# Softmax maxima of a hybrid attention layer: split into two float16 parts before the turn, and turned by a float16 product

## The chip, the cores and the metric

The kernel runs on one core of a Trainium2 chip. The metric is the device time of one execution in microseconds (us), as the median over runs. Before the change it is 2776.42 us, the median of three runs between 2773.62 and 2778.46.

The engines are named as in the profile: PE is TensorE (matrix products; PEld are its weight loads), DVE is VectorE, ACT is ScalarE, POOL is GpSimd, SP is SyncE, which issues most of the transfers. PSUM is the memory that TensorE writes to, in banks of 128 partitions by 512 float32 numbers; SBUF is the main on-chip memory.

## What is computed

The reference is one transformer layer over 2048 tokens of width 1024: a modulated RMS norm, a projection, bidirectional retention beside an attention with 8 query heads and 2 key heads, an output projection, and a feed-forward block. The change lies in the attention alone:

```python
def _dense_attention(q, k, v):
    s = jnp.einsum('bqkgd,bskd->bkgqs', q, k).astype(jnp.float32) * ATT_SCALE
    p = jax.nn.softmax(s, axis=-1).astype(v.dtype)
    return jnp.einsum('bkgqs,bskd->bqkgd', p, v)
```

There are 2304 keys (256 of the context, 2048 of the sequence), head size 64. The softmax subtracts the maximum of each query's scores. The queries and keys are multiplied as split float16 numbers (a high part and the remainder, the low part).

## The kernel before

**Stages.** A first stage (to about 636 us) normalizes and projects the tokens and writes queries, keys and values to memory. The second stage (636 to about 1560 us) is the attention, with the retention, the output projection and the first steps of the feed-forward block between its steps. The third stage (to the end) is the feed-forward block.

**Attention groups.** The attention runs over 32 groups: 16 tiles of 128 queries by 2 key heads, each group with 4 query heads. A group has two passes over the keys.

- *Maxima.* `piece` multiplies queries (as weights, queries on the output's partitions) with 512 keys at a time into a PSUM bank named "mp" (L172, and L176 for the last 256 keys). There are 18 pieces in a group. `maximum` (L185, DVE) reduces each piece to the negated maximum of each query and puts it into the tile "nm". `least` (L191, DVE, twice) takes the minimum of the five parts for each head; it writes the same numbers to columns 64 and 96 of a tile "mt" (queries on partitions, four heads).
- *Turn.* `turn` (L196, PE) transposes "mt" for each of the four heads into an "mp" bank, so that the minima lie along one partition. `rows` (L199, ACT) copies partitions 64 to 127 of that bank as float16, scaled, into the second half of the query tile "qr". `rows2` (L203, DVE) then replaces partitions 96 to 127 by the remainder that float16 had cut off. With them the scores' product subtracts the maximum by itself.
- *Scores and values.* `scores` multiplies 128 keys (as weights) with the 512 queries into a bank "st" (L209 and L210; L210 uses the rows above). `exp` (L215, ACT), `cast` (L219, ACT) and `low` (L226 on POOL or L228 on DVE) make the high and low float16 parts of the probabilities, and `values` (L242, L243) multiplies them with the values.

**Order.** A table of events sets the order. Group n begins its pieces at step k = 18n, one piece a step, and its scores at step k + 22. In each step the phases run in the order scores, piece, maximum, early, exp, cast, low, chain, values and some others for the work between. `least` stands in the chain phase of step k + 18, `turn` in the piece phase of step k + 19 (ahead of the next group's second piece), `rows` in the cast phase of step k + 20 and `rows2` in the early phase of step k + 21. The passes of two groups overlap: while group n turns its minima, group n + 1 makes its first pieces and group n - 1 its last scores.

**Banks.** There are two "mp" banks. Pieces of all groups and the turns share them. A bank is given again when all that reads it is done; which of the two a tile gets is decided when the program is built, by a model of the time. The program's wait for a bank is a semaphore of the engine that read it last.

## Time and profile before

| | |
|---|---|
| median of three runs | 2776.42 us (2773.62 to 2778.46) |
| the profiled execution, first to last instruction (its span, and the only time that the page gives of it) | 2774.9 us |
| TensorE busy | 2657.9 us, 96% |
| VectorE busy | 2103.3 us, 76% |
| ScalarE busy | 1600.3 us, 58% |
| GpSimd busy | 1423.2 us, 51% |
| granted TensorE clock, mean | 0.989 of full speed |

A row of a time line gives the start in us, the duration in us, the engine, the line of the kernel, the operation, the tiles written and read, the sizes, and in brackets how long the engine was idle before and what released it. A row of stretches gives a stretch's bounds and length, then busy time and instructions of PE, PEld, DVE, ACT and POOL, the granted clock, the share of the transfer engines and GB/s. A row of waits gives who waited for what: us in total, times, the longest. Matmuls are pipelined and their ends are modelled, so how long one holds TensorE is read from the start of the next.

### The profile page before, as it was taken

The numbers are of one execution on the slowest core, as the hardware profiler recorded it, in microseconds if no ns is written. First come the engines' busy times: TensorE is split into PE (matmuls) and PEld (weight loads), VectorE is DVE, ScalarE is ACT, GpSimd is POOL, SyncE is SP. The second block draws the span as 40 slices with busy tenths as digits, with TensorE's granted clock in tenths as the row PEclk, the third lists the DMA queues.
The fourth block names the chain that finished last, engine by engine and source line by source line (L and its number), as shares of the span: only waits on it lengthen the run. The fifth ranks groups of instructions, "written<-read, shape, count | busy, mean of one in ns | idle before, by whom it ended". The sixth has DMA issues, their size and how long they took to land.

```text
span 2774.9 us, 45229 instructions
## 1 busy us (share of the span) xinstructions
PE 2657.9 (96%) x16896; PEld 1432.6 (52%) x16896; DVE 2103.3 (76%) x3306; ACT 1600.3 (58%) x2736; POOL 1423.2 (51%) x1182
## 2 busy tenths in 40 slices
PE   7999999888999999999999889999999999999998
PEld 2545654445666666666666544444444444444443
DVE  5857677668877777777777577989999956666676
ACT  3633762227877777787778576555554564434442
POOL 2623772365755657676667644454556721111155
PEclk9999999999999999999999999999999999999999
DMA  7478758584111231322222665665657332222223
GB/s 265 132 251 294 225 167 271 150 265 169 48 60 53 67 96 57 98 79 86 86 76 83 239 209 175 204 190 179 200 187 273 129 108 83 84 89 79 84 76 137
DMA packets 275045, 402.51 MB, mean 145 GB/s; under 512 B 107717, under 2 KB 163141, under 8 KB 272522
## 3 DMA queue, kind: packets, MB, share of 16 engines
q1 hardware_dynamic: 271802, 394.90, 43.9%
q10 hardware_dynamic: 3024, 4.72, 0.5%
q8 instruction: 133, 2.18, 0.3%
q14 instruction: 86, 0.70, 0.1%
HBM read 294.54 MB, written 105.00 MB: 144 GB/s over the span
## 4 chain that ended last, share of the span: by engine, by line
PE 76%; DVE 11%; DMA 4%; issue 3%; ACT 3%; POOL 2%; SPq 0%; POOLq 0%; ACTq 0%; DVEq 0%
PE pd L1894 6%; PE pd L1892 6%; PE pd L1893 6%; PE pu L1715 6%; PE pu L1717 6%; PE pu L1716 6%; PE pso L650 5%; PE pso L651 5%; PE pso L652 5%; PE o L243 3%; PE st L209 3%; PE st L210 3%; PE mp L172 3%; DVE plo L228 2%; DVE nm L185 2%
## 5 line engine op out<-in xcount | busy, mean ns | idle before, releaser
L185 DVE TENSOR_REDUCE nm<-mp 128x1 f32<-128x512 f32 (+1 forms) x576 | 390.3, 685 | 158.6 <-PE mp L172 131.4
L215 ACT ACTIVATE p<-st 128x512 f32<-128x512 f32 x576 | 339.1, 599 | 178.1 <-PE st L210 122.5
L226 POOL TENSOR_TENSOR plo<-p,phi 128x1024 f16<-128x1024 f32 x160 | 351.4, 2197 | 173.2 <-ACT phi L219 141.7
L1715 PE MATMUL pu<-hf,w1f 128*128 128x512 f16 x896 | 341.0, 381 | 7.2 <-ACT w L1732 3.8
L1717 PE MATMUL pu<-hf,w1f 128*128 128x512 f16 x896 | 341.0, 381 | 0.0
L1716 PE MATMUL pu<-hf,w1f 128*128 128x512 f16 x896 | 340.7, 380 | 0.0
L219 ACT ACTIVATE phi<-p 128x1024 f16<-128x1024 f32 x288 | 304.1, 1056 | 0.0
L651 PE MATMUL pso<-wlo,h 128*128 128x512 f16 (+1 forms) x816 | 296.2, 363 | 2.0 <-DVE wlo L548 2.0
L650 PE MATMUL pso<-whi,h 128*128 128x512 f16 (+1 forms) x816 | 296.5, 363 | 1.3 <-ACT whi L547 1.3
L652 PE MATMUL pso<-whi,h 128*128 128x512 f16 (+1 forms) x816 | 296.0, 363 | 0.0
L228 DVE TENSOR_TENSOR plo<-p,phi 128x512 f16<-128x512 f32 x256 | 235.1, 919 | 16.1 <-ACT phi L219 14.9
L242 PE MATMUL o<-wv,plo 128*128 128x65 f16 x2304 | 234.9, 193 | 13.0 <-POOL plo L226 6.6
L243 PE MATMUL o<-wv,phi 128*128 128x129 f16 x2304 | 242.7, 220 | 0.0
L242 PEld LDWEIGHTS <-plo 128*128 128x128 f16 x2304 | 206.1, 98 | 55.6 <-POOL plo L226 15.9
L1918 DVE SCALAR_TENSOR_TENSOR acc<-pd,scv,acc 128x512 f32<-128x512 f32 x248 | 183.1, 743 | 54.0 <-PE pd L1894 51.4
L209 PE MATMUL st<-qr,ks 128*128 128x512 f16 x576 | 219.6, 381 | 4.4 <-ACT p L215 3.8
L210 PE MATMUL st<-qr,ks 128*128 128x512 f16 x576 | 219.7, 381 | 0.1
L243 PEld LDWEIGHTS <-phi 128*128 128x128 f16 x2304 | 205.2, 97 | 21.3 <-issue 0.5
L172 PE MATMUL mp<-ks,qr 128*128 128x512 f16 x512 | 196.1, 383 | 17.2 <-DVE nm L185 17.0
L1680 POOL TENSOR_TENSOR w1s<-w1r 128x512 f32<-128x512 f32 x64 | 92.4, 1444 | 233.4 <-ACT w L1754 159.9
L1892 PE MATMUL pd<-w2t,us 128*128 128x512 f16 x496 | 188.0, 379 | 1.7 <-DVE acc L1918 1.7
L1893 PE MATMUL pd<-w2t,us 128*128 128x512 f16 x496 | 188.0, 379 | 0.0
(377 smaller groups left out, 6109.2 us busy)
## 6 DMA issues: line engine op xcount, KB each, us to landing
w2t<-w2f SPq DMA_DIRECT2D x98, 512.0 KB, 4.2
wm<-in_w_ff SPq DMA_DIRECT2D x64, 512.0 KB, 5.0
w1r<-in_w_ff SPq DMA_DIRECT2D x64, 512.0 KB, 4.7
w2f<-w2f SPq DMA_DIRECT2D x98, 256.0 KB, 2.4
wmr<-in_w_mod SPq DMA_DIRECT2D x32, 512.0 KB, 5.3
w2r<-in_w_ff SPq DMA_DIRECT2D x32, 512.0 KB, 4.2
hf<-hp SPq DMA_DIRECT2D x56, 256.0 KB, 3.5
hf<-hf SPq DMA_DIRECT2D x14, 1024.0 KB, 7.2
```

Source lines behind the costliest of these rows:

```text
L185: nc.vector.tensor_reduce(dst, src, axis=AX.X, op=ALU.max, negate=True)
L226: nc.gpsimd.tensor_tensor(lo, p, hi, op=ALU.subtract)
L242: mm(o[:, : HD + 1], lo[:, i, c], v[:, : HD + 1], start=False, stop=False)
L243: mm(o, hi[:, i, c], v[:, :VW], start=False, stop=last)
L650: mm(self.ps[:, c], hi[:, k], wh, start=k == 0, stop=False)
L651: mm(self.ps[:, c], hi[:, k], wl, start=False, stop=False)
L652: mm(self.ps[:, c], lo[:, k], wh, start=False, stop=k == KT - 1)
L1715: mm(pu[c], whi, hi, start=first and k == 0, stop=False, **more)
L1716: mm(pu[c], whi, lo, start=False, stop=False, **more)
L1717: mm(pu[c], wlo, hi, start=False, stop=k == 3, **more)
L1892: mm(ps, uh, wh, start=first and j == 0, stop=False, **more)
L1893: mm(ps, uh, wl, start=False, stop=False, **more)
```

## The change

The minima are split into a float16 high part and a low part while the queries still lie on partitions, 4 numbers to each partition. `least` now makes three steps on VectorE: one reduction into a small tile "ml", the high part (L192, scaled, rounded to float16 in "mt", column 64), and the low part (L193, the scaled minimum less the high part, column 96). "mt" is a float16 tile, the turn is an ordinary product with a float16 identity, and ScalarE's copy takes both parts at once. `rows2` is gone.

```diff
         def least(self, mt):
             self.mt = mt
             nm = self.nm.rearrange("p a b c -> p (a b) c")
-            for c in (64, 96):
-                nc.vector.tensor_reduce(mt[:, :, c], nm, axis=AX.X, op=ALU.min)
+            m = sm.tile([P, 4], F32, name="ml", tag="ml")
+            nc.vector.tensor_reduce(m, nm, axis=AX.X, op=ALU.min)
+            nc.vector.tensor_scalar_mul(mt[:, :, 64], m, 1 / ROW)
+            nc.vector.scalar_tensor_tensor(mt[:, :, 96], m, 1 / ROW, mt[:, :, 64], op0=ALU.mult, op1=ALU.subtract)
...
             for h in range(4):
-                nc.tensor.transpose(self.m[:, h], self.mt[:, h], ident)
+                mm(self.m[:, h], self.mt[:, h], ident16, start=True, stop=True)
...
-            nc.scalar.activation(self.qr[64:, 1], self.m[64:], AF.Copy, scale=1 / ROW)
-
-        def rows2(self):
-            lo = self.qr[96:, 1]
-            nc.vector.scalar_tensor_tensor(lo, self.m[96:], 1 / ROW, lo, op0=ALU.mult, op1=ALU.subtract)
+            nc.scalar.activation(self.qr[64:, 1], self.m[64:], AF.Copy)
...
+    ident16 = vp.tile([P, P], F16, name="ident16")
+    nc.vector.tensor_copy(ident16, ident)
-    mts = [vp.tile([P, 4, P], F32, name=f"mt{i}") for i in range(2)]
+    mts = [vp.tile([P, 4, P], F16, name=f"mt{i}") for i in range(2)]
...
-        nc.gpsimd.memset(mt[:, :, 80], PSHIFT * math.log(2.0) * HD**0.5)
+        nc.gpsimd.memset(mt[:, :, 80], PSHIFT * math.log(2.0) * HD**0.5 / ROW)
...
             on(k + NK + 2, "cast", g.rows)
-            on(k + NK + 3, "early", g.rows2)
```

Lines behind the diff's first part stand two lower afterwards (L228 is then L226, L226 then L224), and `rows` becomes L201; L191 is then the one reduction, L198 the turn.

The order of VectorE around the 25th turn, before. Rows are in the engine's order; "mt0" is the turned tile, "nm" the maxima, "mp" the banks, and the brackets name the engines whose semaphores a step waits for.

```order
L228 TENSOR_TENSOR plo_17049<-p32_16985,phi_17035 128x512 [waits DVE_49,Pool_49]
L191 TENSOR_REDUCE mt0_6849<-nm_16616 128x4 [waits DVE_49]
L191 TENSOR_REDUCE mt0_6849<-nm_16616 128x4
L185 TENSOR_REDUCE nm_17039<-mp_17043 128x1 [waits PE_49]
L228 TENSOR_TENSOR plo_17049<-p32_16985,phi_17035 128x512
L185 TENSOR_REDUCE nm_17039<-mp_17079 128x1 [waits PE_49]
L1543 TENSOR_TENSOR u_17103<-bank1_17092,a2_302 128x512 [waits DMAHW7_49,PE_49]
L1386 TENSOR_TENSOR oat_17130<-bank0_17087,dT_318 128x512
L185 TENSOR_REDUCE nm_17039<-mp_17100 128x1 [waits PE_49]
L203 SCALAR_TENSOR_TENSOR qr_16298<-mp_17074,qr_16298 32x512 [waits DMAHW0_49,Activation_49]
```

The same place after the change:

```order
L226 TENSOR_TENSOR plo_17075<-p32_17011,phi_17061 128x512 [waits DVE_49,Pool_49]
L191 TENSOR_REDUCE ml_17077<-nm_16641 128x4 [waits DVE_49]
L192 TENSOR_SCALAR mt0_6851<-ml_17077 128x4 [waits DVE_49]
L193 SCALAR_TENSOR_TENSOR mt0_6851<-ml_17077,mt0_6851 128x4 [waits DVE_49]
L185 TENSOR_REDUCE nm_17065<-mp_17069 128x1 [waits PE_49]
L226 TENSOR_TENSOR plo_17075<-p32_17011,phi_17061 128x512
L185 TENSOR_REDUCE nm_17065<-mp_17107 128x1 [waits PE_49]
L1542 TENSOR_TENSOR u_17131<-bank1_17120,a2_302 128x512 [waits DMAHW7_49,PE_49]
L1385 TENSOR_TENSOR oat_17158<-bank0_17115,dT_318 128x512
L185 TENSOR_REDUCE nm_17065<-mp_17128 128x1 [waits PE_49]
```

The two reductions, of which the second waited for nothing, became three steps that each wait for the one before (DVE's own semaphore); L203 is gone from behind the third maximum.

TensorE at the same turn, before: the turn, the first piece behind it ("mp_17079"), and the second and third ("mp_17100", "mp_17138").

```order
L196 MATMUL mp_17074<-ident_60,mt0_6849 128x128 [waits DVE_49,PE_49]
L196 MATMUL mp_17074<-ident_60,mt0_6849 128x128 x3
L172 MATMUL mp_17079<-ks_315,qr_16742 128x512 [waits DVE_49]
...
L172 MATMUL mp_17100<-ks_315,qr_16742 128x512 [waits DVE_49]
...
L172 MATMUL mp_17138<-ks_315,qr_16742 128x512 [waits DVE_49]
```

After the change:

```order
L198 MATMUL mp_17102<-ident16_6849,mt0_6851 128x128 [waits PE_49]
L198 LDWEIGHTS mt0_6851
L198 MATMUL mp_17102<-ident16_6849,mt0_6851 128x128
...
L172 MATMUL mp_17107<-ks_315,qr_16768 128x512 [waits DVE_49]
...
L172 MATMUL mp_17128<-ks_315,qr_16768 128x512 [waits Activation_49]
...
L172 MATMUL mp_17166<-ks_315,qr_16768 128x512
```

The second piece behind the turn now waits for ScalarE, the copy out of the turn's bank, and no longer for VectorE's maximum of the first piece. This is so at 25 of the 31 turns that have pieces behind them; at the other 6 the second piece still waits for VectorE and the third for ScalarE. The rest of the order of ScalarE, GpSimd and SyncE is the same.

## The prediction

> **What bounds the kernel now.** I read the page's head first, then the stretch of the attention stage, then what TensorE waits for in it, and last the time line around single turns.

> ```profile
> span 2774.9 us, 45229 instructions
> PE 2657.9 (96%) x16896; PEld 1432.6 (52%) x16896; DVE 2103.3 (76%) x3306; ACT 1600.3 (58%) x2736; POOL 1423.2 (51%) x1182
> 636.00:1520.00 884.00, 845.16 (x7913) 558.84 (x7913) 702.27 (x1233) 685.03 (x1115) 587.57 (x441) 0.99 0.25 79
> PE mp L172 <- DVE nm L185: 15.6, 23, 2.6
> PE o L242 <- DVE plo L228: 5.6, 9, 1.2
> PE o L242 <- POOL plo L226: 4.8, 7, 1.7
> PE mp L196 <- DVE mt L191: 2.6, 4, 0.7
> ```

> The third line is the stretch in which all 32 turns lie: 884.0 us, of which TensorE is busy 845.2, VectorE 702.3, ScalarE 685.0 and GpSimd 587.6. TensorE sets the pace; what the other engines save counts only where TensorE waits for them. The last four lines are those waits. The longest, L172 for L185, lies mostly right behind a turn. Here is the 14th, first TensorE, then ScalarE and VectorE:

> ```profile
> 989.38 0.60 PE L196 MATMUL mp<-ident,mt 128*128 128x128 f32 x4
> 989.82 0.38 PE L172 MATMUL mp<-ks,qr 128*128 128x512 f16 x1
> 990.25 0.38 PE L210 MATMUL st<-qr,ks 128*128 128x512 f16 x1
> 990.98 0.38 PE L172 MATMUL mp<-ks,qr 128*128 128x512 f16 x1 [0.35 <-DVE nm L185]
> 990.21 0.59 ACT L199 ACTIVATE qr<-mp 64x512 f16<-64x512 f32 x1
> 990.24 0.69 DVE L185 TENSOR_REDUCE nm<-mp 128x1 f32<-128x512 f32 x1 [0.49 <-PE mp L172]
> ```

> The four transposes hold TensorE for 989.82 - 989.38 = 0.44 us. The turn keeps one of the two "mp" banks until L203 has read it, so the second piece behind it (990.98) goes to the bank of the first piece and must wait for that piece's maximum (990.24 + 0.69 = 990.93). Going through all 32 turns in this way (from start to start on TensorE), I count about 14 us lost at the second piece.

> **The change, part by part.** *The turn on TensorE.* No row shows an fp16 product of 128 columns. The nearest is the pair of L242 (65 columns) and L243 (129):

> ```profile
> 1547.67 0.19 PE L242 MATMUL o<-wv,plo 128*128 128x65 f16 x1
> 1547.70 0.22 PE L243 MATMUL o<-wv,phi 128*128 128x129 f16 x1
> 1547.76 0.19 PE L242 MATMUL o<-wv,plo 128*128 128x65 f16 x1
> 1548.37 0.38 PE L209 MATMUL st<-qr,ks 128*128 128x512 f16 x1
> ```

> L243 holds TensorE for 1547.76 - 1547.70 = 0.06 us, its weight load beside it. So four products take about 0.23 us for 0.44, 0.21 less a turn; the other end is the fp32 rate, no gain, and nothing speaks for a loss. I take the L243 row: its type is that of the new product, its columns one more. At most 32 x 0.21 = 6.7 us, but only where nothing else holds the next piece. [...]

> *The minima on VectorE.* Before, two independent reductions; after, three steps that each wait for the one before.

> ```profile
> L191 DVE TENSOR_REDUCE mt<-nm x64: 157/166/175, 636.4 to 1518.2; 128x4 f32<-128x20 f32 x64
> L203 DVE SCALAR_TENSOR_TENSOR qr<-mp,qr x32: 696/697/698, 640.5 to 1522.3; 32x512 f16<-32x512 f32 x32
> 92.66 0.17 DVE L1034 TENSOR_SCALAR lgp<-lgp 128x8 f32<-128x8 f32 x1
> 92.86 0.17 DVE L1033 TENSOR_TENSOR lgp<-lgp,dw 128x8 f32<-128x8 f32 x1
> 93.06 0.17 DVE L1034 TENSOR_SCALAR lgp<-lgp 128x8 f32<-128x8 f32 x1
> ```

> Dependent small steps start 0.20 us apart. The pair of L191 takes 0.25 us in all (the 25th turn below shows 0.24); the new chain takes 0.20 + 0.20 + 0.17 = 0.57, so the turn's operand is ready 0.32 us later. Queued behind it on VectorE is the maximum of the first piece of the next group, for whose bank TensorE's next L172 waits. In 9 turns TensorE waits for the chain already, and the 0.32 us comes back there; in the others there are 0.3 us or more to spare.

> *A lock that the new chain meets.* Its last step reads two SBUF operands (the minimum and the high part); neither L191 nor L203 (one operand in PSUM) does. What that can cost, a tiny step of the same kind shows:

> ```profile
> L1526 DVE TENSOR_TENSOR ss<-ss x16: 130/159/2058, 792.0 to 1596.7; 128x1 f32<-128x1 f32 x16
> 1360.63 2.06 DVE L1526 TENSOR_TENSOR ss<-ss 128x1 f32<-128x1 f32 x1
> 1360.55 2.13 POOL L226 TENSOR_TENSOR plo<-p,phi 128x1024 f16<-128x1024 f32 x1
> ```

> A step of 0.16 us lasted 2.06 because GpSimd's L226 had started 0.08 us earlier; it ended with L226. L191 never left 157 to 175 ns. [...] I laid the new step (0.40 us behind the first L191) over GpSimd's rows at each turn: in 7 of 32 it falls into a running GpSimd step that lasts another 0.6 to 0.9 us. The 25th turn:

> ```profile
> 1307.76 0.24 DVE L191 TENSOR_REDUCE mt<-nm 128x4 f32<-128x20 f32 x2
> 1308.05 1.03 POOL L1356 TENSOR_TENSOR okw<-ork,kd 128x512 f32<-128x512 f32 x1
> 1308.15 0.63 PE L196 MATMUL mp<-ident,mt 128*128 128x128 f32 x4 [0.70 <-DVE mt L191]
> ```

> The new step would start at 1308.16 and wait until 1309.08, so this turn moves by 0.92 + 0.32 = 1.24 us.

> *L203 goes, the bank is free earlier.* L203 is 0.70 us of VectorE in each turn, 22.3 us in all, but VectorE is idle 884.0 - 702.3 = 181.7 us of the stretch. What counts is the bank. The order shows that in most turns the second piece now takes the turn's own bank and waits for ScalarE's copy (in the 14th: 990.21 + 0.59 = 990.80, 0.13 us ahead of the maximum; and the copy itself starts 0.21 earlier). Where the copy comes late, the scheduler left the old wait in place (6 turns). The largest loss of all, in the 26th turn, shows what is late next:

> ```profile
> 1340.18 2.46 DVE L228 TENSOR_TENSOR plo<-p,phi 128x512 f16<-128x512 f32 x1
> 1342.56 0.68 DVE L185 TENSOR_REDUCE nm<-mp 128x1 f32<-128x512 f32 x1
> 1343.29 0.59 PE L172 MATMUL mp<-ks,qr 128*128 128x512 f16 x1 [2.61 <-DVE nm L185]
> 1344.95 0.26 PE L242 MATMUL o<-wv,plo 128*128 128x65 f16 x1
> ```

> The piece no longer waits for 1343.24. The next values product, which started at 1344.95, needs the L228 that ends at 1342.64, and 0.32 us later behind the longer chain: it can start at about 1343.0, 1.9 us earlier, and no more.

> *The sum at the start of the values product behind each turn.* Fourteen turns in which the chain has room: 0.11 to 0.33 us earlier each, -3.1 us. Nine in which the chain is waited for or nearly: the eight without the 26th together +0.8, the 26th -1.9. Seven blocked by GpSimd: from -0.8 to +1.2 (the 25th), together +3.2. The last turn has no pieces behind it: 0. The first turn is covered:

> ```profile
> 640.47 0.70 DVE L203 SCALAR_TENSOR_TENSOR qr<-mp,qr 32x512 f16<-32x512 f32 x1
> 641.32 0.58 PE L209 MATMUL st<-qr,ks 128*128 128x512 f16 x1 [0.24 <-DMA qr<-aq]
> ```

> The first scores wait for the queries' transfer (641.32), not for L203 (641.17). The transfer hides both the gain there and the new identity's cast, once 0.2 us (by L1034's row); without it the first turn would be some 0.5 us later. Together -1.0 us. Other pieces that wait for L185 find VectorE 0.70 - 0.32 us less busy in each group: the total of that wait is 15.6 us, most of it at the turns, so I take -0.5 us, between 0 and -2.

> *The clock.* After two of the long waits TensorE ran at half clock:

> ```profile
> 663.66:667.07 3.41, 1.26 (x13) 0.62 (x11) 2.94 (x3) 1.70 (x3) 1.66 (x1) 1.00 0.00 0
> 667.07:670.48 3.41, 3.41 (x21) 1.76 (x19) 1.94 (x3) 1.34 (x3) 2.12 (x1) 0.50 0.02 5
> 1339.50:1342.91 3.41, 1.18 (x8) 0.65 (x7) 3.41 (x4) 3.14 (x8) 2.13 (x1) 1.00 0.63 137
> 1342.91:1346.32 3.41, 3.03 (x21) 1.93 (x21) 1.71 (x3) 1.36 (x2) 1.92 (x1) 0.50 0.91 286
> ```

> Stretches of 3.41 us in which TensorE was busy 1.26 and 1.18 us are followed by one at a granted clock of 0.50, which costs up to 1.7 us each. The waits there shrink to about 1.5 us but do not go. I count one of the two as gone, -1.7 us, with ends 0 and -3.4. Sum: -1.0 - 0.5 - 1.7 = -3.2 us. The profiled execution's span of 2774.9 us lies 1.5 below the median of 2776.42, within the three runs (2773.62 to 2778.46), so I take the sum off the median: 2773 us.

> **The rivals.** *The gain comes in full.* If GpSimd's steps shift so that the new step seldom meets one, the seven blocked turns give what the others do and the sum at the turns is -5.3; with -0.5 and one to two half-clock stretches (-1.7 to -3.4) that is about -8, 2768 us. For it: the blocked steps are 0.6 to 0.9 us from being free, and the order around them moves. Against it: GpSimd is busy 587.6 of 884.0 us. Chance 0.34.

> *Slower by the lock.* The same busy share, 0.66, would put 21 of 32 turns under a GpSimd step if the seven I count are luck. Each blocked turn costs 4.3 / 7 = 0.6 us net (the sum with it, -1.0, less the sum without, -5.3, over seven). From 19 on the loss outweighs the gains by 0.2%: 19 x 0.6 = 11.4 against 5.3 + 0.5 + 5.5. At 21, with both half-clock stretches left, it is 12.6 - 5.3 - 0.5 = +6.8 us, 2783 us. Chance 0.11.

> *The product is no faster than the transpose.* Then the fourteen free turns give nothing: -3.2 + 2.9, 2776 us. Its chance, 0.05, is in the 0.55 for no measurable change.

> **How the numbers follow.** About 0.2%, 5.5 us, is what a measurement of this kernel can tell from no change (its three runs spread over 4.8). The forecast, 2773, with the rival at 2776, has 0.55 and lies within it; the full gain, 0.34, is faster; the lock, 0.11, is slower. The range leaves out the far tenth of the one and most of the other: 2766 to 2781 us.

> **What would show it.** Right: the four L198 start 0.06 us apart and hold TensorE 0.23 us; L191 to L193 start 0.20 us apart in most turns, and in about 7 the last lasts 0.6 us or more with a GpSimd step beside it; the wait of L172 for L185 falls to some 5 us, and waits for ScalarE's copy and for the turn's operand appear, 3 to 7 us each; one half-clock stretch is left. Wrong: L193 blocked in 15 turns or more, or hardly ever; the products at 0.11 us; or the gain found outside the 884 us.

## The result: 0.36% slower

| | before | after |
|---|---|---|
| median of four runs each | 2777.06 us (2773.62 to 2778.46) | 2786.08 us (2785.47 to 2788.93) |
| ratio, with its 95% interval | | 1.0036 (1.0023 to 1.005) |
| start of the first and of the last turn | 636.80, 1519.35 | 636.53, 1527.41 |
| from the first to the last turn | 882.55 us | 890.88 us |

The forecast of 2773 us was wrong, and the time lies outside its range. Nearly the whole loss lies between the first turn and the last: 8.3 us more there, against 8.9 us more in the span (2783.8 for 2774.9). One execution among all those below (e13, 6322 us) is a slow one and enters no ratio. The page's head after the change:

```profile
span 2783.8 us, 45173 instructions
PE 2649.6 (95%) x16896; PEld 1424.7 (51%) x16896; DVE 2104.5 (76%) x3307; ACT 1598.2 (57%) x2736; POOL 1418.7 (51%) x1182
```

The stretch that holds the 32 turns:

```profile
636.00:1528.00 892.00, 839.17 (x7913) 551.51 (x7914) 708.69 (x1229) 683.66 (x1115) 584.03 (x441) 0.99 0.26 78
```

And what TensorE waits for in it (us in total, times, the longest; the prediction's rows count from 640 us, and from there on the first two totals are 12.1 and 11.0):

```profile
PE mp L198 <- DVE mt L193: 13.1, 12, 2.7
PE mp L172 <- DVE nm L185: 12.3, 26, 2.2
PE o L240 <- DVE plo L226: 9.3, 14, 1.3
PE mp L172 <- ACT qr L201: 1.1, 3, 0.4
```

TensorE works 6.0 us less in the stretch (839.2 for 845.2), as it should, and yet the stretch is 8.0 us longer. Counted from 640 us in both, the turn's wait for its operand has risen from 2.6 to 12.1 us, and the values' wait for VectorE's low part (L226, before L228) from 5.6 to 9.3. The pieces' wait for the maximum fell by only 4.6 us, from 15.6 to 11.0. VectorE lost the 22.3 us of L203, but is as busy as before (2104.5 for 2103.3): something in it takes longer. The three new steps, as minimum, median and longest in ns:

```profile
L191 DVE TENSOR_REDUCE ml<-nm x32: 156/164/170, 516.6 to 1526.2; 128x4 f32<-128x20 f32 x32
L192 DVE TENSOR_SCALAR mt<-ml x32: 175/177/1046, 636.0 to 1526.4; 128x4 f16<-128x4 f32 x32
L193 DVE SCALAR_TENSOR_TENSOR mt<-ml,mt x32: 176/177/2111, 636.2 to 1526.6; 128x4 f16<-128x4 f32 x32
```

The reduction never varies; each of the others is sometimes many times as long. The fifth turn, GpSimd and VectorE in order of time, then the turn on TensorE:

```profile
731.05 1.72 POOL L1424 TENSOR_TENSOR oo<-oo,ogate 128x512 f32<-128x512 f32 x1
731.57 0.16 DVE L191 TENSOR_REDUCE ml<-nm 128x4 f32<-128x20 f32 x1
731.76 1.05 DVE L192 TENSOR_SCALAR mt<-ml 128x4 f16<-128x4 f32 x1
732.80 2.12 POOL L224 TENSOR_TENSOR plo<-p,phi 128x1024 f16<-128x1024 f32 x1
732.84 2.11 DVE L193 SCALAR_TENSOR_TENSOR mt<-ml,mt 128x4 f16<-128x4 f32 x1
735.01 0.61 PE L198 MATMUL mp<-ident,mt 128*128 128x128 f16 x4 [2.56 <-DVE mt L193]
```

L192 has one SBUF operand, and was not on my list of steps that can be blocked. It is held until GpSimd's L1424 ends (731.05 + 1.72 = 732.77). By then GpSimd's next step is ready and starts at 732.80. L193 needs L192's result, comes at 732.84 and loses again, this time for a whole GpSimd step. A chain of 0.59 us takes 3.38 (731.57 to 734.95). No L191 lasted over 0.17 us in the 32 turns; why a step of L192's form can be held, the rows don't show.

The blocked turns and how long the two steps lasted, in us (0.18 where nothing blocks):

| turn | 5th | 19th | 23rd | 25th | 27th | 29th | 31st |
|---|---|---|---|---|---|---|---|
| L192 | 1.05 | 0.93 | 0.93 | 0.18 | 0.81 | 0.81 | 0.81 |
| L193 | 2.11 | 1.19 | 1.19 | 0.95 | 0.18 | 0.18 | 0.97 |

These are the seven turns that the prediction counted. Over 0.18 us the steps add up to 4.3 us at L192 and 5.5 at L193. In four of the six turns with a held L192, L193 is held as well. Behind two of these turns TensorE then ran at half clock:

```profile
731.54:734.95 3.41, 0.91 (x13) 0.42 (x10) 3.34 (x5) 1.67 (x3) 3.35 (x2) 1.00 0.00 0
734.95:738.36 3.41, 3.35 (x22) 2.10 (x23) 2.57 (x5) 1.89 (x3) 0.00 (x0) 0.50 0.00 0
1137.73:1141.14 3.41, 0.84 (x8) 0.65 (x9) 3.34 (x6) 1.81 (x3) 3.41 (x4) 1.00 0.38 79
1141.14:1144.55 3.41, 3.41 (x25) 2.25 (x24) 3.41 (x4) 2.04 (x3) 2.77 (x2) 0.50 0.03 7
```

Both half-clock stretches of before (667.07 and 1342.91) are gone; these two, at the 5th and the 19th turn, took their place.

A second loss has no new step in it. At the 11th turn VectorE's subtraction L228 (after: L226) is an old step with two SBUF operands, right behind the chain and the first maximum. Before, it came 0.13 us ahead of GpSimd's L226:

```profile
901.95 0.68 DVE L228 TENSOR_TENSOR plo<-p,phi 128x512 f16<-128x512 f32 x1
902.08 2.54 POOL L226 TENSOR_TENSOR plo<-p,phi 128x1024 f16<-128x1024 f32 x1 [3.59 <-DVE xr L1512]
```

After the change the longer chain makes it 0.20 us late instead, and the next maximum and the second piece wait behind it:

```profile
903.89 2.12 POOL L224 TENSOR_TENSOR plo<-p,phi 128x1024 f16<-128x1024 f32 x1 [3.59 <-ACT phi L217]
904.09 2.47 DVE L226 TENSOR_TENSOR plo<-p,phi 128x512 f16<-128x512 f32 x1
906.49 0.68 DVE L185 TENSOR_REDUCE nm<-mp 128x1 f32<-128x512 f32 x1
907.22 0.38 PE L172 MATMUL mp<-ks,qr 128*128 128x512 f16 x1 [2.18 <-DVE nm L185]
```

Whichever starts second waits: before, it was GpSimd's step, 2.54 us for 2.12; after, VectorE's, 2.47 us for 0.68. Such a VectorE step of over 2 us stands behind 2 turns before and behind 9 after, of which three (the 19th, the 25th and the 31st) are turns whose chain was itself held. So there were two theories of a lock (on the new steps, the lock theory of the expectations; on the old step that now comes late, called the race below), and as rivals the longer way to the operand by itself (the chain or operand theory), and the bank or the product (the bank theory).

### The profile page after: what moved, and what is told of

Read it like the earlier page. It is cut to its first block, busy times and chain, and to the rows that moved or that the text cites. A ratio compares the mean times of both kernels' runs of the same rounds, so it can differ in the third digit from the quotient of the medians.

```text
span 2783.8 us, 45173 instructions
## 1 busy us (share of the span) xinstructions
PE 2649.6 (95%) x16896; PEld 1424.7 (51%) x16896; DVE 2104.5 (76%) x3307; ACT 1598.2 (57%) x2736; POOL 1418.7 (51%) x1182
## 3 DMA queue, kind: packets, MB, share of 16 engines
q8 instruction: 133, 2.18, 0.3%
## 4 chain that ended last, share of the span: by engine, by line
PE 77%; DVE 11%; ACT 3%; DMA 3%; issue 3%; POOL 2%; SPq 0%; POOLq 0%; ACTq 0%; DVEq 0%
PE pu L1714 6%; PE pu L1715 6%; PE pu L1716 6%; PE pd L1893 6%; PE pd L1891 6%; PE pd L1892 6%; PE pso L648 5%; PE pso L649 5%; PE pso L650 5%; PE o L241 3%; DVE plo L226 3%; PE st L207 3%; PE st L208 3%; PE mp L172 3%; DVE nm L185 2%
## 5 line engine op out<-in xcount | busy, mean ns | idle before, releaser
L185 DVE TENSOR_REDUCE nm<-mp 128x1 f32<-128x512 f32 (+1 forms) x576 | 389.2, 684 | 159.7 <-PE mp L172 132.2
L224 POOL TENSOR_TENSOR plo<-p,phi 128x1024 f16<-128x1024 f32 x160 | 349.6, 2186 | 173.1 <-ACT phi L217 132.6
L226 DVE TENSOR_TENSOR plo<-p,phi 128x512 f16<-128x512 f32 x256 | 248.6, 972 | 19.0 <-ACT phi L217 17.8
L172 PE MATMUL mp<-ks,qr 128*128 128x512 f16 x512 | 195.1, 381 | 13.8 <-DVE nm L185 12.3
```

The costliest lines, as they stand in the source:

```text
L185: nc.vector.tensor_reduce(dst, src, axis=AX.X, op=ALU.max, negate=True)
L224: nc.gpsimd.tensor_tensor(lo, p, hi, op=ALU.subtract)
```

## Experiments

Line numbers shift by a few between the kernels. In all of them the order of ScalarE, GpSimd and SyncE is that of the kernel they are made from; TensorE's follows the banks of before where L203 stands, of after where it doesn't. Each ratio is against the kernel before on the same chip. The expectations of e1 to e4 are in us and go by the 2777 us of before in the table above; on the chip of these four, before takes 2772.7 us, so they are to be compared as ratios.

| kernel | ratio, 95% interval | first to last turn, us |
|---|---|---|
| after | 1.0036 (1.0023 to 1.005) | 890.9 |
| e1: four reductions | 0.9996 (0.9987 to 1.0004) | 878.7 |
| e2: last step alone can be blocked | 1.0010 (1.0001 to 1.0018) | 881.5 |
| e3: high part alone | 0.9983 (0.9974 to 0.9992) | 877.8 |
| e4: before, two steps that can be blocked | 1.0106 (1.0091 to 1.0122) | 908.1 |
| e5: before, two reductions instead | 1.0056 (1.0044 to 1.0069) | 899.1 |
| e6: after again | 1.0030 (1.0020 to 1.0041) | 892.1 |
| e7: e3 with float32 transposes | 0.9983 (0.9974 to 0.9992) | 876.8 |
| e8: e3 with L203 and its bank | 0.9986 (0.9977 to 0.9995) | 876.3 |
| e9: e3, two reductions behind the operand | 0.9998 (0.9989 to 1.0008) | 881.8 |
| e10: e8, two reductions behind the operand | 1.0038 (1.0025 to 1.0051) | 893.8 |
| e11: after without L193 | 1.0004 (0.9995 to 1.0013) | 881.9 |
| e12: e11 with a reduction for L192 | 0.9989 (0.9981 to 0.9998) | 878.7 |
| e13: before, one reduction for two | 0.9999 (0.9990 to 1.0008) | 882.9 |

The last column is from one profiled execution each, the start of the last turn less that of the first (before: 882.6).

**e1: the same two parts by reductions alone.**

```diff
-            m = sm.tile([P, 4], F32, name="ml", tag="ml")
-            nc.vector.tensor_reduce(m, nm, axis=AX.X, op=ALU.min)
-            nc.vector.tensor_scalar_mul(mt[:, :, 64], m, 1 / ROW)
-            nc.vector.scalar_tensor_tensor(mt[:, :, 96], m, 1 / ROW, mt[:, :, 64], op0=ALU.mult, op1=ALU.subtract)
+            m = sm.tile([P, 4, 2], F32, name="ml", tag="ml")
+            nc.vector.tensor_reduce(mt[:, :, 64], nm, axis=AX.X, op=ALU.min)
+            nc.vector.tensor_reduce(m[:, :, 0], nm, axis=AX.X, op=ALU.min)
+            nc.vector.tensor_reduce(m[:, :, 1], mt[:, :, 64:65], axis=AX.X, op=ALU.min, negate=True)
+            with nc.allow_low_precision(reason="low part"):
+                nc.vector.tensor_reduce(mt[:, :, 96], m, axis=AX.X, op=ALU.add)
...
-    nc.vector.tensor_copy(ident16, ident)
+    nc.vector.tensor_scalar_mul(ident16, ident, 1 / ROW)
...
-        nc.gpsimd.memset(mt[:, :, 80], PSHIFT * math.log(2.0) * HD**0.5 / ROW)
+        nc.gpsimd.memset(mt[:, :, 80], PSHIFT * math.log(2.0) * HD**0.5)
```

> The same two parts are formed by four reductions on VectorE and nothing else (no step with two SBUF operands, none of the form of L192); the scale 1/ROW sits in the identity. The order on TensorE, ScalarE, GpSimd and SyncE is that of the changed kernel. Lock theory (both L192 and L193 lose to GpSimd's steps, and that is the whole loss): no step of the chain lasts over 0.25 us, the turn's product waits some 4 us in all instead of 14.5, the two half-clock stretches behind the long waits are gone, 2771 to 2777 us. Chain theory (the operand is ready later because three dependent steps stand where two independent ones stood): this chain is 0.1 us longer still, so 2786 us or more. Bank theory (the second piece waits for ScalarE's copy, or the product itself costs): nothing of that changes, 2784 to 2788 us.

Measured: 0.9996. The last step:

```profile
L195 DVE TENSOR_REDUCE mt<-ml x32: 172/174/177, 632.8 to 1511.1; 128x4 f16<-128x8 f32 x32
```

And the turn's wait for it:

```profile
PE mp L200 <- DVE mt L195: 4.0, 6, 0.9
```

No step of the chain is long any more, the wait is 4.0 us, and from 641 us to the last turn there is no half-clock stretch. The loss of 0.30 to 0.36% is gone, though this chain is longer: the new steps' lock is the loss. By the chain theory or the bank theory it would have stayed. But e1 is only level with before: what the change was to gain is not there either.

**e2: only the last step can be blocked.** A second reduction of the maxima, which doesn't wait for the first, makes the high part in place of L192; the difference (`tensor_tensor`) has two SBUF operands. The scale is in the identity, as in e1.

```diff
             m = sm.tile([P, 4], F32, name="ml", tag="ml")
+            nc.vector.tensor_reduce(mt[:, :, 64], nm, axis=AX.X, op=ALU.min)
             nc.vector.tensor_reduce(m, nm, axis=AX.X, op=ALU.min)
-            nc.vector.tensor_scalar_mul(mt[:, :, 64], m, 1 / ROW)
-            nc.vector.scalar_tensor_tensor(mt[:, :, 96], m, 1 / ROW, mt[:, :, 64], op0=ALU.mult, op1=ALU.subtract)
+            nc.vector.tensor_tensor(mt[:, :, 96], m, mt[:, :, 64], op=ALU.subtract)
...
```

> L192 becomes a reduction that doesn't depend on the first; only the last step, with two SBUF operands, can be blocked. This is the case that the prediction priced: one blocked step in about 7 turns, 0.6 to 0.9 us each. Lock theory with two steps in a row (the second loses because the first was held until GpSimd started its next step): the last step is blocked for the rest of one GpSimd step only, never for two, and the time falls by more than half of the loss, 2777 to 2780 us. Lock theory with the last step alone at fault: 2785 us, as the changed kernel. Chain theory: the chain is 0.1 us shorter, 2784 us. Bank theory: 2784 to 2788 us.

Measured: 1.0010.

```profile
L193 DVE TENSOR_TENSOR mt<-ml,mt x32: 176/178/966, 633.2 to 1514.1; 128x4 f16<-128x4 f32 x32
```

Its longest is 0.97 us (six turns, 0.73 to 0.97), never a whole GpSimd step of 2.1; the two reductions ahead of it last 0.18 us at most. This is the lock that the prediction priced, at 4.3 us, and it costs 0.14% over e1, 3.9 us. The rest of the change's lock, 0.20 to 0.26%, comes with L192: its own hold, and the second collision of L193 that follows from it.

**e11 and e12: L192 alone.** In e11 only L193 and the low part are taken out; in e12 a reduction also takes L192's place.

> The changed kernel without L193: one reduction and L192, the step with one SBUF operand; the low part is left out. If a step of L192's form alone can lose to GpSimd: it lasts 0.8 to 1.05 us in 5 or 6 turns (730, 1138, 1254, 1376, 1436 and 1496 us in the changed kernel), and the time is 2 to 5 us above the same chain in reductions. If only steps with two SBUF operands are blocked and L192's delays in the changed kernel came from its neighbour: all at 0.18 us, the same time as the chain in reductions.

> Control for the last: the high part by two dependent reductions (the second in L192's place; the low part is left out), as long a chain (0.38 us) and nothing that can be blocked. Race theory: 0.13 us more of VectorE than before the change, which is about the margin by which L228 came ahead of GpSimd in the turn at 902 us, so between one and five of the lost races: 0.9983 to 0.9995. Operand theory: 0.9983 to 0.9988.

Measured: 1.0004 and 0.9989. The second fits the race's range and, by its interval, the operand's too: e12 serves as a control alone. In e11:

```profile
L192 DVE TENSOR_SCALAR mt<-ml x32: 176/177/1043, 634.8 to 1516.1; 128x4 f16<-128x4 f32 x32
```

A step with one SBUF operand on four numbers is blocked by itself, in the same six turns as in the change; 0.15% between the two, some 4 us. L192 alone and L193 alone (e2) thus cost 0.15 and 0.14%, the two in a row 0.34 to 0.40%. That this is more than their sum is what the second collision leads one to expect (behind a held L192, L193 is held for 4.7 us in all), but with intervals of some 0.1% to each side the times alone don't show the size of that share.

**e4 and e5: the same steps in the kernel before.** Two steps whose results nobody reads stand between the two reductions of L191: in e4 of the forms of L192 and L193, in e5 two reductions.

> The kernel before, with two more steps between its two reductions, of the forms of L192 and L193, whose results nobody reads; the transposes, L203 and the banks stay. Lock theory: some 5 to 9 turns have a step blocked for 0.5 to 2.1 us, 2782 to 2788 us. Chain theory (0.4 us later in the 9 turns that wait for the chain): 2780 to 2781 us. Bank theory: 2777 to 2778 us.

> Control for the kernel before with two more steps: the same two places, but both steps are reductions, which have not been blocked in any run so far. The chain is as long, nothing can lose to GpSimd. Lock theory: of the 29 us that the two steps cost there, at least 12 (the lock's cost in the first turn-to-last-turn stretch of the changed kernel) go, and no half-clock stretch follows a long wait: 1.001 to 1.006 of the kernel before. Chain theory: nothing of it goes, 1.009 to 1.011.

Measured: 1.0106 and 1.0056. The first lies far above what any of the theories gave. The difference between the two, half a per cent, is the lock:

```profile
L193 DVE SCALAR_TENSOR_TENSOR ml<-mt,ml x32: 161/164/2107, 635.0 to 1542.6; 128x4 f16<-128x4 f32 x32
```

The other half I had not foreseen when I wrote e4's ranges: two reductions of 0.16 us, of which the first never lasts over 163 ns, cost 0.56%, 15.5 us, in 32 turns. The 1.0056 lies within what e5's lock theory allowed, but its sign does not: four half-clock stretches (from 689.9, 908.3, 1085.8 and 1355.5 us) follow long waits, where none was expected. So "the lock on the new steps is all" does not hold in this kernel, and that led to the race. By itself e5 doesn't tell the race from the later operand: the turn's wait for it rises too, from 2.6 to 5.2 us.

**e6: after again.**

> The changed kernel again, beside the others on one chip: 1.0025 to 1.005 of the kernel before, the same seven turns blocked, L192 over 0.25 us in 6 and L193 in 5 of them, whatever the theory; if the blocked turns were luck of one execution, other turns or another number of them.

Measured: 1.0030, with the same longest steps (1048 and 2110 ns) in the same seven turns. The collisions are the program's, not one execution's luck. The clock is in part luck: behind the 25th turn e6 has a third half-clock stretch, after one in which TensorE was busy 1.56 of 3.41 us; in the first execution TensorE was busy 1.71 us in the stretch at that place, and no half clock followed.

**e3, e9: the operand, or what stands behind it.** e3 has one reduction into the float16 tile (scale in the identity, no low part); e9 adds two dependent reductions behind it (the edit is that from e3 to e9).

```diff
             nc.vector.tensor_reduce(mt[:, :, 64], nm, axis=AX.X, op=ALU.min)
+            d = sm.tile([P, 2, 4], F16, name="ml", tag="ml")
+            nc.vector.tensor_reduce(d[:, 0], mt[:, :, 64:65], axis=AX.X, op=ALU.min)
+            nc.vector.tensor_reduce(d[:, 1], d[:, 0].unsqueeze(2), axis=AX.X, op=ALU.min)
```

> The minimum is kept as its high part alone, by one reduction; the low part (row 96 of the rows) is left out and stays zero. Lock theory: as with four reductions, and up to 3 us less for the shorter chain, 2768 to 2775 us. Chain theory: the operand is ready 0.1 us earlier than before the change, so the whole gain of the shorter turn and of L203 shows, 2766 to 2770 us. Bank theory: 2783 to 2787 us.

> The high part alone (the low part is left out), and behind it two more dependent reductions of four values that nobody reads. TensorE's operand is ready as early as with the high part alone; what stands behind on VectorE comes 0.4 us later, as in the changed kernel where nothing is blocked. Race theory (what costs is that VectorE's subtraction L228 right behind the turn comes just after GpSimd's L226 instead of just ahead of it, and then waits for it): that step lasts over 2 us in 7 to 9 turns instead of 2, and 2 to 4 us come back: 0.9989 to 0.9998 of the kernel before. Operand theory (what costs is the later operand of the turn): no change, 0.9980 to 0.9987.

Measured: 0.9983 and 0.9998. The operand is ready as early in both (TensorE waits for it 1.9 us in all in either). The 11th turn in e3:

```profile
900.13 0.68 DVE L223 TENSOR_TENSOR plo<-p,phi 128x512 f16<-128x512 f32 x1
900.27 2.52 POOL L221 TENSOR_TENSOR plo<-p,phi 128x1024 f16<-128x1024 f32 x1 [3.60 <-DVE xr L1508]
```

And in e9:

```profile
898.20 2.13 POOL L224 TENSOR_TENSOR plo<-p,phi 128x1024 f16<-128x1024 f32 x1 [3.59 <-ACT phi L217]
898.39 2.49 DVE L226 TENSOR_TENSOR plo<-p,phi 128x512 f16<-128x512 f32 x1
901.53 0.38 PE L172 MATMUL mp<-ks,qr 128*128 128x512 f16 x1 [2.18 <-DVE nm L185]
```

VectorE comes 0.14 us first in the one and 0.19 us late in the other. The subtraction is over 2 us behind 2 turns in e3 and behind 6 in e9 (7 to 9 were expected), as in e1, which is as fast as e9. The race theory holds, the operand theory doesn't: 0.15%, 4 us, for 0.4 us of VectorE that TensorE's operand never sees. The lost races are not worth the same: in the profiled executions e9 is 4.0 us behind e3 at the last turn, and 3.9 of them arise between the 11th turn and the 12th, with the wait of 2.18 us above and a half-clock stretch behind it (from 902.2). Over the rest of the way the two are even; e3 has two half-clock stretches of its own, both before 700 us.

**e7, e8, e10: the product and the bank.** e7 is e3 with "mt" in float32 and the transposes of before. e8 is e3 with `rows2` back. e10 is e8 with e9's two reductions.

> The high part alone (the low part, row 96, is left out), but through the float32 transposes of before: the bank is free as early as with the product, only the product's gain is missing. If the shorter turn is worth what was forecast (0.21 us in some 14 to 20 turns), 3 to 4 us above the kernel with the high part alone: 0.9993 to 1.0000. If that gain is swallowed by other waits: 0.998 to 0.999, as there.

> The high part alone (the low part is left out) through the float16 product, but L203 of before stands again: it reads the turn's bank late and holds VectorE 0.70 us in each turn (it works on zeros). If the earlier bank and VectorE's time are worth something (forecast: the second piece's wait for L185 falls from 15.6 us to some 5): 3 to 8 us above the kernel with the high part alone, 0.9995 to 1.001. If other waits take that place: 0.998 to 0.999.

> The same two reductions in the kernel that keeps L203 and the late bank (high part alone, float16 product). Race theory with the bank: the second piece behind the turn then waits for a maximum that stands behind the blocked subtraction, in some six turns by 1.4 to 2.3 us, and half-clock stretches come with it: 8 to 12 us above the same kernel without the two steps, 1.0015 to 1.0035 of the kernel before. If the earlier bank is worth nothing in such turns either: 0.999 to 1.0 as with the early bank. Operand theory: 0.9983 to 0.999.

Measured: 0.9983, 0.9986 and 1.0038, the last a little above its range. With the short chain it makes no difference whether the product or the early bank is there. With the long one the bank (with L203's 0.70 us of VectorE) matters: e10 lies 0.52% above e8, e9 only 0.15% above e3. The 18th turn shows how. After the change:

```profile
1109.95 2.48 DVE L226 TENSOR_TENSOR plo<-p,phi 128x512 f16<-128x512 f32 x1
1111.39 0.38 PE L172 MATMUL mp<-ks,qr 128*128 128x512 f16 x1
```

In e10:

```profile
1109.95 2.51 DVE L230 TENSOR_TENSOR plo<-p,phi 128x512 f16<-128x512 f32 x1
1113.11 0.38 PE L172 MATMUL mp<-ks,qr 128*128 128x512 f16 x1 [1.53 <-DVE nm L185]
```

The same lost race; the second piece takes the turn's bank in the one, and in the other waits 1.7 us longer for a maximum behind the blocked subtraction. So the change's early bank did work: it hid most of the races that the change's own chain lost. It is also the likely reason for e5's loss, as e5 has the late bank.

**e13: the kernel before with one reduction for two.**

```diff
-            for c in (64, 96):
-                nc.vector.tensor_reduce(mt[:, :, c], nm, axis=AX.X, op=ALU.min)
+            nm = bc(nm.unsqueeze(2), [P, 4, 2, 5])
+            nc.vector.tensor_reduce(mt[:, :, 64:128:32], nm, axis=AX.X, op=ALU.min)
```

> The kernel before, whole, with one reduction in place of the two of L191: it reads the maxima twice (a repeated dimension) and writes both columns of the turned tile. Transposes, L203, banks and the order of every engine stay. If what the three kernels with the high part alone gain (0.9983 to 0.9986) comes from what they have in common with this one, the VectorE steps ahead of the turn taking 0.17 instead of 0.25 us: 0.9980 to 0.9992. If it comes from the product, the early bank or the missing low part: 0.9996 to 1.0004.

Measured: 0.9999. It saves 0.06 us of the 0.25 a turn (one step of 0.19), and that is worth nothing. The gain of e7 and e8 is thus not from their shorter chain: the float16 product alone (e8) and the early bank alone (e7) earn about 0.15% each. Together (e3) they earn no more; a sum, 0.997, lies outside e3's interval, though by less than the sum's own uncertainty. e3 is among the fastest versions tried, 3.9 us under before on its chip, but it leaves the low part out; no version with both parts was found faster than before.

## Why the prediction was wrong, point by point

**Right: the turn on TensorE.** The 14th turn:

```profile
991.22 0.18 DVE L193 SCALAR_TENSOR_TENSOR mt<-ml,mt 128x4 f16<-128x4 f32 x1
992.47 0.39 PE L198 MATMUL mp<-ident,mt 128*128 128x128 f16 x4
992.70 0.38 PE L172 MATMUL mp<-ks,qr 128*128 128x512 f16 x1
```

The products hold TensorE 992.70 - 992.47 = 0.23 us, as taken. The chain's length where nothing blocks it, 0.57, was right too (0.58 to 0.59). That the first turn would not count was right in the sum: the first scores come 1.7 us later behind the first turn (6.23 us for 4.52), but at the third turn the kernel is 1.4 us ahead.

**Wrong, and the step that failed: "A lock that the new chain meets".** The number of blocked turns was right, seven; their price was not. The step asked whether one instruction, L193, falls into a GpSimd step, and let it wait for that step's end. It left out L192, for having one SBUF operand, though no row had shown that only steps with two are held, and so it missed the second collision: in four of six turns L192, released by the end of one GpSimd step, handed over to L193 just after the next GpSimd step had started. The seven turns were priced at 4.3 us for the lock (+3.2 with their gains); the lock measures 0.34 to 0.40% (1.0030 and 1.0036 against e1's 0.9996), 9 to 11 us, with the half-clock stretches and the three late subtractions behind held chains in it. Where the last step alone was held (e2, 0.97 us at its longest), the price was right: 3.9 us. At the 25th turn, where only L193 was caught, the wait to that step's end came about as taken: 0.92 us foreseen, 0.95 - 0.18 = 0.77 measured.

**Wrong as well: the sum without the lock.** Even with the one lock that was priced, the forecast would have missed: e2 is 0.10%, 2.8 us, above before, not 3.2 below. Two things make up the difference: a loss that is not in the sum (the race, next), and gains that came out smaller. Without the lock the sum gives 7.5 us; e3, which has no held step and no more late subtractions than before, gained 0.17%, 4.7 us.

**Missing: the race behind the chain.** "Queued behind it on VectorE is the maximum of the first piece" was right, but I priced the delay only as TensorE sees it ("0.3 us or more to spare"). Behind that maximum stands a step that GpSimd can hold, and for it 0.3 us decided between going first and waiting 2 us. The rows of before held it: 901.95 against 902.08. By e9 against e3 the longer queue costs 4 us with the early bank; by e10 against e8, 14 us without.

**Half right: the bank.** The second piece does take the turn's bank. The wait of L172 for L185 fell to 11.0 us, not to 5, since the lost races put new waits there; and the 26th turn did gain (its 2.61 us are gone).

**Wrong in size: the clock.** Both half-clock stretches of before went, one more than counted, and two new ones (three in e6) came from the blocked turns.

**The rivals.** "Slower by the lock" had the right mechanism, but made it depend on more blocked turns (19 or more) instead of longer ones. "The gain in full", 8 us, came in no kernel: e1, the whole change without a lock on the new steps, gained 1, and the kernels without the low part 4 to 5. "The product is no faster than the transpose" was wrong on TensorE (0.23 us for 0.44), but e7 and e3 show that with the early bank the time is the same with either.

## What to carry to other kernels

Before a small VectorE step is put on a critical chain, ask of each step whether its form can be held by a running GpSimd instruction, not only of those with two SBUF operands (L192, with one, lasted up to 1.05 us here for 0.18); and look whether the step behind a held one meets the next GpSimd step, as it did here in four turns of six. Steps that were not held in these runs (reductions, 0.20 us at most) kept the same chain free of this: with four of them the kernel takes 0.9996 of the time before, with one and the two that were held 1.0036. And a delay on an engine's queue is also to be laid over the next contended step behind it: a margin of 0.13 us in the trace of before was worth 2 us of waiting at one turn (the 11th: VectorE's step took 2.47 us for 0.68).

## What the runs showed of the hardware

- A `TENSOR_SCALAR` from SBUF to SBUF, on 4 numbers for each partition, lasted up to 1.05 us beside GpSimd's steps, for 0.18 otherwise; no `TENSOR_REDUCE` of the chains lasted over 0.20 us in any of these kernels.
- Of VectorE's subtraction (two SBUF operands) and GpSimd's, the one that starts second waits: at the 11th turn 2.54 us for GpSimd's instead of 2.12 when it came 0.13 us late, 2.47 us for VectorE's instead of 0.68 when it came 0.20 us late.
- A long wait need not bring half clock. In e8 TensorE waits longer at the 26th turn than it did before, and the clock stays:

```profile
1342.81 0.38 PE L172 MATMUL mp<-ks,qr 128*128 128x512 f16 x1 [2.83 <-DVE nm L185]
```

The two stretches of 3.41 us around that wait:

```profile
1338.28:1341.69 3.41, 1.71 (x18) 0.96 (x16) 3.41 (x5) 3.36 (x8) 2.12 (x1) 1.00 0.52 122
1341.69:1345.10 3.41, 2.29 (x24) 1.46 (x24) 2.46 (x4) 1.98 (x4) 1.18 (x1) 1.00 0.82 253
```
